# Output rows fetched and split by two threads, column groups in a new order, the bonus a thread of its own, value transposes of full width

## The chip, the cores and the metric

The kernel runs on one core of one Trainium2 chip. The metric is device time in microseconds of one execution; lower is better. A core has TensorE (PE; weight loads are shown apart as PEld), VectorE (DVE), ScalarE (ACT), GpSimd (POOL) and SyncE (SP), whose queue issues the DMAs here. The engines run side by side, each its own instructions in a fixed order, and wait for one another through semaphores.

## The reference, cut to what matters

One layer works on 528 prompt tokens (16 of them meta tokens) and 8 short sequences of 8 tokens, 592 rows of 2048 columns in all. One projection feeds two branches:

```python
z = einsum('btd,dn->btn', x, w_in)            # 4 x 1024 + 128 columns (r,k,v,g, lora), then 4 x 1024 (q,k,v,g)
# branch A, 16 heads of 64 (RWKV-7), zs = z shifted and mixed:
S = S * w_t + sa (x) b_t + v_t (x) k_t ;  o_t = S r_t      # sa = S (-kk_t)
bonus = sum(r * k * r_k) * v
o_a = (group_norm(o) + bonus) * silu(g)
# branch B, 8 heads of 128 (retention): scores with decay, a state by blocks, group norm, silu gate
h = einsum('btc,cd->btd', concat(o_a, o_b), w_out)
y = layer_norm(ALPHA * x + h)
```

The final states and the last projected rows are outputs too. All is float32.

## The kernel before, in words

**Planner.** No order is written out by hand. Each piece of work is a Python generator (a "job") that records operations; `Order` keeps a clock for each engine, prices every operation (`Engine.cost`, `TensorEngine`), and decides when it is emitted. The projection and output matmuls are emitted in a plain loop; behind each of them `pump` looks through the jobs by priority and emits those operations whose data are ready by the planner's clocks. For TensorE, data of other engines count as ready `LAG + SLACK` after their end (`SLACK` = 100 ns). `ensure` and `force` emit whatever is next when the loop needs something that is not there yet. So prices and slack only move instructions; they are no instructions themselves.

**Projection.** Rows of the input stand transposed in XH (leading part) and XL (rest), weights are split alike into wh and wl, and each product is three matmuls (wh by XH, wh by XL, wl by XH). A unit is 128 columns of `w_in`; it has two halves of tokens (272, 258 or 256, then 320), each 48 matmuls into one of two banks (`pj`). The list `units` has a first unit L (lora), then for each of 8 pairs p (two A heads, one B head): A k r v g, B q k v g. `gen_evac` empties the banks in that order, one half after the other, and waits there until the pair before has read the buffer that it writes. Splitting weights is ACT (wh) and DVE (wl), by `gen_split`.

**A heads.** `gen_a(p)` makes decays (a DVE scan, line 673), keys and the products within chunks of 64 tokens (ten chunks; the two heads' halves of the array side by side), then transposes k, then v chunk by chunk: ten transposes of 64 columns (line 760), with three evictions for each group of chunks. It then makes the bonus (`BD` products, added into zsV), and only then waits for the inverse of `gen_u(p)` (through DRAM: lt_d, tt_d) and runs the recurrence `gen_c` over nine chunks: three products a step, with evictions between. `gen_s(p)` is the part of the short sequences, `gen_f(p)` the normalization, bonus, gate and the row's write to o_d. **B heads** are `gen_b(h)`.

**Output.** The rows of o_d are fetched into five buffers (TH, E1, E2, TA, Z0 in turn), split into xo and xl (in the place of XH and XL) by `gen_o`, and multiplied with `w_out` in 64 steps. The first 14 steps take two token tiles only (six matmuls of 512 columns). `gen_o` is one thread: it waits once for the last pair (inverse, state products, bonus, evictions), then in turn splits row k and fetches row k+5.

## Time and profile before

| | |
|---|---|
| three runs | 1344.74, 1345.04, 1347.03 us (median 1345.04) |
| the profiled execution | 1345.04 us, its span 1343.3 us |
| busy | PE 1309.4 us, PEld 1230.2, DVE 879.8, ACT 634.4, POOL 55.3 |
| DMA | 139.82 MB, mean 104 GB/s |

The span runs from the first to the last instruction of the program; about 1.7 us lie around it. Busy is the union of an engine's instructions. A float32 matmul leaves two records, a split product or a transpose one. Matmuls are pipelined: the record of one overlaps the next, so the cost of one is the distance between starts, and an idle time of TensorE shows only where it is longer than that overlap. PE and DVE operations are recorded through helpers, so nearly all have the lines 380 (DVE, ACT, POOL), 403 (matmul), 409 (transpose) and 420 (DMA issue); in the changed kernel these are two lines further down.

### The profile page before, as it was taken

How to read it: one execution, taken by the hardware profiler on the slowest of the kernel's cores; microseconds unless marked ns; L12 is line 12 of the kernel's file. 1: busy time of each engine (PE TensorE's matmuls, PEld its weight loads, DVE VectorE, ACT ScalarE, POOL GpSimd, SP SyncE). 2: the span in 40 equal slices, each digit the busy share in tenths (PEclk: the TensorE clock that was granted, in tenths of full speed). 3: DMA queues.
4: the chain of work that ended last, by engine and by line, in shares of the span. 5: the costliest groups of instructions: out<-in, count | busy, mean ns of one | idle time of the engine just before them, and what ended most of it. 6: DMA issues, size and time to landing. Idle time of an engine off the chain costs nothing.

```text
span 1343.3 us, 27153 instructions
## 1 busy us (share of the span) xinstructions
PE 1309.4 (97%) x10488; PEld 1230.2 (92%) x10488; DVE 879.8 (65%) x2168; ACT 634.4 (47%) x1505; POOL 55.3 (4%) x117
## 2 busy tenths in 40 slices
PE   6999999999999999999999999999999998999995
PEld 6999999999999999999999999999999995777774
DVE  5765587658765876587658765876587658634258
ACT  4543654365536553655365536553655375512110
POOL 0000010000000010001000100010001000000002
PEclk9999999999999999999999999999999999999998
DMA  8343234322433243324332433243324356563224
GB/s 244 89 110 84 68 89 120 83 82 74 119 84 83 74 116 86 84 74 114 87 84 74 113 88 85 73 113 86 86 74 114 83 162 191 172 193 118 79 67 145
DMA packets 232344, 139.82 MB, mean 104 GB/s; under 512 B 58668, under 2 KB 212102, under 8 KB 231238
## 3 DMA queue, kind: packets, MB, share of 16 engines
q1 hardware_dynamic: 232214, 138.08, 36.2%
q8 instruction: 82, 1.34, 0.4%
q14 instruction: 48, 0.39, 0.1%
HBM read 119.30 MB, written 18.74 MB: 103 GB/s over the span
## 4 chain that ended last, share of the span: by engine, by line
PE 92%; DVE 5%; issue 1%; ACT 1%; DMA 0%; DVEq 0%; SPq 0%; ACTq 0%
PE bank L403 88%; PE bank L409 4%; DVE RW L380 3%; DVE wl L380 1%; DVE XL L380 1%; DMA RW<-in_x_prompt_dram 0%; DVE SHT L380 0%; ACT XH L380 0%; DVE XH L380 0%; ACT RT L380 0%; DVE RT L380 0%; ACT RSv L380 0%; ACT wh L380 0%; ACT SF L380 0%; ACT RHS L380 0%
## 5 line engine op out<-in xcount | busy, mean ns | idle before, releaser
L403 PE MATMUL bank<-XL,wh 128*128 128x320 f32 (+3 forms) x2080 | 631.3, 303 | 0.0
L403 PE MATMUL bank<-XH,wh 128*128 128x320 f32 (+3 forms) x2080 | 629.6, 303 | 1.2 <-ACT wh L380 1.2
L403 PE MATMUL bank<-XH,wl 128*128 128x320 f32 (+3 forms) x2080 | 626.1, 301 | 0.6 <-DVE wl L380 0.6
L403 PEld LDWEIGHTS bank<-XH,wh 128*128 128x128 f32 x2080 | 391.8, 188 | 3.6 <-ACT wh L380 1.4
L403 PEld LDWEIGHTS bank<-XH,wl 128*128 128x128 f32 x2080 | 392.0, 188 | 2.9 <-DVE wl L380 0.8
L403 PEld LDWEIGHTS bank<-XL,wh 128*128 128x128 f32 x2080 | 391.8, 188 | 2.9
L380 DVE TENSOR_TENSOR wl<-raw,wh 128x512 fp32r<-128x512 f32 x292 | 200.8, 689 | 156.2 <-ACT wh L380 151.8
L380 ACT ACTIVATE wh<-raw 128x512 fp32r<-128x512 f32 x292 | 183.8, 630 | 172.9 <-PE bank L403 145.6
L380 DVE TENSOR_TENSOR RW<-RW 120x84 f32<-120x84 f32 (+26 forms) x544 | 137.9, 256 | 18.5 <-DMA RW<-lt_d 4.1
L403 PE MATMUL bank<-RW 32*32 32x32 f32 (+6 forms) x2000 | 137.0, 239 | 4.8 <-DVE RW L380 4.7
L403 PEld LDWEIGHTS bank<-RW 32*32 32x32 f32 (+4 forms) x2000 | 109.8, 144 | 23.5 <-DVE RW L380 9.7
L380 ACT ACTIVATE RW<-bank 64x256 f32<-64x256 f32 (+8 forms) x218 | 93.2, 438 | 52.8 <-PE bank L403 29.1
L380 ACT ACTIVATE RT<-bank 64x320 f32<-64x320 f32 (+9 forms) x122 | 47.7, 397 | 114.0 <-DVE RT L380 72.6
L403 PE MATMUL bank<-more,XH 128*128 128x512 f32 (+1 forms) x250 | 75.9, 395 | 0.0
L380 ACT ACTIVATE SF<-RW,FT 64x64 f32<-64x64 f32 x144 | 49.4, 343 | 54.7 <-DVE RW L380 52.9
L403 PE MATMUL bank<-wh,XH 128*128 128x512 f32 x157 | 61.8, 396 | 0.0
L403 PE MATMUL bank<-wl,XH 128*128 128x512 f32 (+1 forms) x157 | 61.7, 395 | 0.0
L409 PE MATMUL bank<-CT,RW 128*128 128x128 f32 (+2 forms) x348 | 53.4, 283 | 8.3 <-DMA RW<-in_x_prompt_dram 7.6
L403 PEld LDWEIGHTS bank<-more,XH 128*128 128x128 f32 (+1 forms) x250 | 45.6, 183 | 12.6
L380 ACT ACTIVATE RW<-bank,OMM 128x272 f32<-128x272 f32 (+1 forms) x66 | 33.3, 504 | 45.6 <-PE bank L403 42.9
L403 PE MATMUL bank<-wh,XL 128*128 128x512 f32 x126 | 50.4, 400 | 1.4 <-DVE XL L380 1.4
L409 PEld LDWEIGHTS bank<-CT,RW 128*128 128x128 f32 (+2 forms) x348 | 42.0, 140 | 9.5 <-issue 7.6
(151 smaller groups left out, 1352.9 us busy)
## 6 DMA issues: line engine op xcount, KB each, us to landing
raw<-in_w_in_dram SPq DMA_DIRECT2D x259, 256.0 KB
raw<-in_w_out_dram SPq DMA_DIRECT2D x48, 256.0 KB
CT<-in_w_out_dram SPq DMA_DIRECT2D x30, 256.0 KB
RT<-in_state_ret_dram SPq DMA_DIRECT2D x8, 512.0 KB
out_dram<-RT SPq DMA_DIRECT2D x8, 512.0 KB
RW<-in_x_prompt_dram SPq DMA_DIRECT2D x16, 256.0 KB
out_dram<-RW SPq DMA_DIRECT2D x16, 256.0 KB
RW<-o_d SPq DMA_DIRECT2D x14, 288.0 KB
```

Of the source, the lines that this page charges most:

```text
L380: self.order.submit(Op(self.key, self.cost(name, n, kw, psum), reads, [out], lambda: f(*args, **kw)))
L403: lambda: self.eng.matmul(out, lhsT, rhs, start=start, stop=stop), (passes, move, load, shape, tiles)))
L409: lambda: self.eng.transpose(out, in_, ident), (1, move, _cols(in_) / 1.2, shape, tiles)))
```

## The change

- **Value transposes.** Five transposes of 128 columns (two chunks at a time) in two groups instead of ten of 64 in three; the chunks then lie in the two halves of the partitions, and each group is emptied by six evictions.
- **Bonus.** It becomes the job X{p}, started behind the transposes; the recurrence no longer waits for it. Readers wait for it: the addition in `gen_f` and the eviction of the next pair's r. A new mark V{p} tells the state part that the values are in place.
- **Column groups.** Ak Ar Bq Bk Bv Bg Av Ag, in the last pair Ak Ar Bq Av Bk Bv Ag Bg.
- **Fetch and split.** `gen_fetch` issues each row's fetch when its own buffer is free (TH, E1, E2 after the inverse, TA after the state products, Z0 after all evictions), `gen_o` splits.
- **Planner.** SLACK 200; a DVE operation costs 82 instead of 68 ns ahead of its elements, a scan twice as much per element, ACT 68 and 107 instead of 51 and 93.
- `gen_shift` also waits for all evictions.

```diff
@@ -29,7 +29,7 @@
 NPAIR = 8
 RAW_BUFS = 3
 HI_BUFS = 4
-SLACK = 100.0
+SLACK = 200.0
 AHEAD = -300.0
 RUN = 1200.0
 DRAIN = 90.0
@@ -44,6 +44,8 @@
 TURN = (4, 0, 1, 2, 3)
 LATE = 5
 EARLY = 14
+TURNS = "Ak Ar Bq Bk Bv Bg Av Ag"
+TURNS_LAST = "Ak Ar Bq Av Bk Bv Ag Bg"
 KEEP = ("A", 7, "g")
 BACKLOG = {0: 4000.0, 1: 1000.0, 2: 500.0, 3: 300.0, 4: 100.0}
 
@@ -356,10 +358,10 @@
 
     def cost(self, name, n, kw, psum):
         if self.key == "DVE":
-            return 68 + n * (6.3 if name == "reciprocal" else 1.04) + 57 * sum(
+            return 82 + n * {"reciprocal": 6.3, "tensor_tensor_scan": 2.08}.get(name, 1.04) + 57 * sum(
                 _is_ap(kw.get(k)) for k in ("scalar", "scalar1", "scalar2"))
         if self.key == "ACT":
-            return (51 if psum else 93) + n * 0.833 + 93 * sum(_is_ap(kw.get(k)) for k in ("scale", "bias"))
+            return (68 if psum else 107) + n * 0.833 + 93 * sum(_is_ap(kw.get(k)) for k in ("scale", "bias"))
         if kw.get("op") == ALU.pow:
             return 150 + n * 190.0
         if name == "memset":
@@ -752,16 +754,27 @@
         yield from prev(("F", 99))
         G.memset(Y[0:64, 0, 9, :], 0.0)
         G.memset(Y[64:128, 1, 9, :], 0.0)
-        for c0, c1 in ((0, 4), (4, 8), (8, 10)):
+        for g0, g1 in ((0, 4), (4, 5)):
             bb, = yield from take()
-            b = bb.rearrange("p (c n) -> p c n", c=4)
-            n = c1 - c0
-            for c in range(c0, c1):
-                T.transpose(b[0:64, c - c0, :], zsV[:, 64 * c:64 * c + 64], ident)
-            act(ZZ[64:128, c0:c1], b[0:64, 0:n].rearrange("p c (h v) -> p c h v", h=2))
-            act(Y[64:128, 0, c0:c1, :], b[0:64, 0:n, 0:64])
-            act(Y[0:64, 1, c0:c1, :], b[0:64, 0:n, 64:128])
+            b = bb.rearrange("p (g n) -> p g n", g=4)
+            for g in range(g0, g1):
+                T.transpose(b[:, g - g0, :], zsV[:, 128 * g:128 * g + 128], ident)
+            for e in range(2):
+                own, cs = b[64 * e:64 * e + 64, 0:g1 - g0], slice(2 * g0 + e, 2 * g1, 2)
+                act(ZZ[64:128, cs], own.rearrange("p g (h v) -> p g h v", h=2))
+                act(Y[64:128, 0, cs, :], own[:, :, 0:64])
+                act(Y[0:64, 1, cs, :], own[:, :, 64:128])
             give(bb)
+        mark(f"V{p}", 1)
+        od.call(lambda: od.start(f"X{p}", gen_bonus(p), 2))
+        yield from until((f"U{p}", 99))
+        b, = yield from take()
+        yield from gen_c(p, b)
+        give(b)
+        od.call(lambda: od.start(f"F{p}", gen_f(p), 2))
+        yield
+
+    def gen_bonus(p):
         yield from hold()
         b0, b1 = yield from take(2)
         for b, (c0, n) in zip((b0, b1), halves):
@@ -773,13 +786,6 @@
             tt(zsV[:, c0:c0 + n], b[:, :n], zsV[:, c0:c0 + n])
         release()
         give(b0, b1)
-        mark(name, 3)
-        yield
-        yield from until((f"U{p}", 99))
-        b, = yield from take()
-        yield from gen_c(p, b)
-        give(b)
-        od.call(lambda: od.start(f"F{p}", gen_f(p), 2))
         yield
 
     def gen_c(p, b):
@@ -879,6 +885,7 @@
                 if e == 0:
                     act(on[ro, 512:576], tr[0:64, 64 * h:64 * h + 64], ACTF.Identity, sc[ri], bi[ri])
         give(tr)
+        yield from until((f"X{p}", 99))
         tt(on, on, zsV[:, 64:640], ALU.add)
         stt(on, on, 0.5, zsG[:, 64:640])
         if p < NPAIR - 1:
@@ -908,6 +915,7 @@
                         m4[64 * e:64 * e + 64, :, 2 * h + r, :])
         T.transpose(n0[:, 256:384], RSv.rearrange("p r b t -> p (r b t)"), ident)
         act(RSs, n0[:, 256:384])
+        yield from until((f"V{p}", 1))
         mm(n0[:, 384:512], AR_[:, 1728:1856], Y[:, :, 9, :])
         tt(RHSs[0:64, 0:64], n0[0:64, 384:448], RSs[0:64, 0:64], ALU.add)
         tt(RHSs[64:128, 64:128], n0[64:128, 448:512], RSs[0:64, 64:128], ALU.add)
@@ -1060,7 +1068,7 @@
                         mark("lora", 1)
                 elif kind == "A":
                     if half == 0 and p:
-                        yield from until((f"A{p-1}", 1 if s == "k" else 3) if s in "kr" else (f"F{p-1}", 99))
+                        yield from until({"k": (f"A{p-1}", 1), "r": (f"X{p-1}", 99)}.get(s, (f"F{p-1}", 99)))
                     zs, i = {"r": (zsR, 0), "k": (zsK, 1), "v": (zsV, 2), "g": (zsG, 3)}[s]
                     evac_shift(units[ui], zs, 8 * i + p, half, b)
                 else:
@@ -1094,7 +1102,7 @@
 
     units = [("L", 0, "")]
     for p in range(NPAIR):
-        units += [("A", p, s) for s in "krvg"] + [("B", p, s) for s in "qkvg"]
+        units += [(x[0], p, x[1]) for x in (TURNS if p < NPAIR - 1 else TURNS_LAST).split()]
 
     def col0(u):
         kind, p, s = u
@@ -1263,26 +1271,37 @@
         obank = [(sq, pj[0], pj[1], r0, r1, m0, m1, ob)[i % 8] for i in range(len(cells))]
         trows = lambda t: 128 if t < 4 else 64
 
+        def gen_fetch():
+
+            for i in range(KO - 2):
+                t, kt = otk[i % 5], korder[i]
+                if t is TA:
+                    yield from until((f"S{NPAIR-1}", 1))
+                elif t is Z0:
+                    yield from until(("evac", 2 * len(units)))
+                else:
+                    yield from until((f"U{NPAIR-1}", 2))
+                if i >= 5:
+                    yield from until(("o", i - 4))
+                yield from until((f"{'F' if kt < 8 else 'B'}{kt % 8}", 99))
+                S.dma_start(out=t[:, 0:576], in_=o_d[kt])
+                mark("fetch", i + 1)
+                yield
+
         def gen_o():
 
-            yield from until((f"U{NPAIR-1}", 2), (f"S{NPAIR-1}", 1), (f"A{NPAIR-1}", 3), ("evac", 2 * len(units) - 8))
-
-            for ki in range(KO + 5):
-                if ki >= 5:
-                    k = ki - 5
+            for k in range(KO):
+                if k < KO - 2:
+                    yield from until(("fetch", k + 1))
                     t = otk[k % 5][:, 0:576]
-                    if k >= KO - 2:
-                        yield from until((f"B{NPAIR-1}", 99), (f"{'F' if k == KO - 1 else 'B'}{NPAIR-1}", 99))
-                        t = Y_[:, 64:640] if k == KO - 1 else ron
-                    yield from until(("event", n_in - 4 + min(3, (640 * k + 639) // TOK // 4) + 1))
-                    act(xo[:, k, 0:576], t)
-                    tt(xl[:, k, 0:512], t[:, 0:512], xo[:, k, 0:512].bitcast(F32), ALU.subtract)
-                    tt(xo[:, k, 576:640], t[:, 512:576], xo[:, k, 512:576].bitcast(F32), ALU.subtract)
-                    mark("o", k + 1)
-                if ki < KO - 2:
-                    kt = korder[ki]
-                    yield from until((f"{'F' if kt < 8 else 'B'}{kt % 8}", 99))
-                    S.dma_start(out=otk[ki % 5][:, 0:576], in_=o_d[kt])
+                else:
+                    yield from until((f"X{NPAIR-1}", 99), (f"B{NPAIR-1}", 99), (f"{'F' if k == KO - 1 else 'B'}{NPAIR-1}", 99))
+                    t = Y_[:, 64:640] if k == KO - 1 else ron
+                yield from until(("event", n_in - 4 + min(3, (640 * k + 639) // TOK // 4) + 1))
+                act(xo[:, k, 0:576], t)
+                tt(xl[:, k, 0:512], t[:, 0:512], xo[:, k, 0:512].bitcast(F32), ALU.subtract)
+                tt(xo[:, k, 576:640], t[:, 512:576], xo[:, k, 512:576].bitcast(F32), ALU.subtract)
+                mark("o", k + 1)
 
         def gen_xin():
             yield from until((f"F{NPAIR-1}", 99))
@@ -1337,7 +1356,7 @@
         xsamp_y = y_sample.rearrange("b t d -> (b t) d")
 
         def gen_shift():
-            yield from until((f"B{NPAIR-1}", 99))
+            yield from until((f"B{NPAIR-1}", 99), ("evac", 2 * len(units)))
             rows = SHO.rearrange("p s i -> p (s i)")
             for g, (c0, n) in enumerate(((0, 33), (33, 88), (121, 88), (209, 88))):
                 T.transpose(r0[0:n, 128 * g:128 * g + 128], rows[:, c0:c0 + n], ident)
@@ -1353,6 +1372,7 @@
             S.dma_start(out=lnb, in_=ln_b[0].partition_broadcast(128))
             yield
 
+        od.start("fetch", gen_fetch(), OPRIO)
         od.start("o", gen_o(), OPRIO)
         od.start("shift", gen_shift(), 4)
         od.start("ln", gen_ln(), 4)
```

TensorE has 40 instructions fewer (9072 for 9112); all others are the same in number and kind, in another order. Three places follow.

VectorE, fifth pair, around the scan of the decays (RW<-CT,RW 128x657). N is the eviction that the recurrence's next product waits for, wl a weight split. Before:

```order
L380 TENSOR_SCALAR RW<-RW 128x657
L380 SCALAR_TENSOR_TENSOR RT<-RT 128x576
L380 SCALAR_TENSOR_TENSOR RW<-CT,RW 128x657
L380 COPY MID<-RW 128x9
L380 TENSOR_TENSOR RW<-RW,MID 128x585
L380 TENSOR_TENSOR wl_107<-raw_100,wh_103 128x512
L380 TENSOR_TENSOR RW<-bank_118,N_78 64x128
L380 TENSOR_TENSOR wl_108<-raw_101,wh_104 128x512
```

Now:

```order
L382 TENSOR_SCALAR RW<-RW 128x657
L382 SCALAR_TENSOR_TENSOR RW<-CT,RW 128x657
L382 TENSOR_TENSOR wl_108<-raw_101,wh_104 128x512
L382 COPY MID<-RW 128x9
L382 TENSOR_TENSOR RW<-RW,MID 128x585
L382 TENSOR_TENSOR RW<-bank_118,N_78 64x128
L382 TENSOR_TENSOR wl_109<-raw_99,wh_105 128x512
```

The split has moved from behind the scan's followers to right behind the scan; an operation of the B head (RT) no longer stands ahead of it.

TensorE, fifth pair, the products within chunks (bank<-RW) among projection matmuls. Before:

```order
L403 MATMUL bank_118<-RW 128x128
L403 MATMUL bank_119<-RW 128x128
L403 MATMUL bank_115<-XH,wh_105 128x272
L403 MATMUL bank_118<-RW 128x128
L403 MATMUL bank_119<-RW 128x128
L403 MATMUL bank_118<-RW 128x128
L403 MATMUL bank_115<-XL,wh_105 128x272
```

Now:

```order
L405 MATMUL bank_116<-XH,wl_108 128x320
L405 MATMUL bank_119<-RW 128x128
L405 MATMUL bank_118<-RW 128x128
L405 MATMUL bank_119<-RW 128x128
L405 MATMUL bank_118<-RW 128x128
L405 MATMUL bank_119<-RW 128x128
L405 MATMUL bank_118<-RW 128x128
L405 MATMUL bank_119<-RW 128x128
L405 MATMUL bank_118<-RW 128x128
L405 MATMUL bank_116<-XH,wh_104 128x320
```

The first piece shows the last two of five, one projection matmul and the remaining three; now eight stand together.

TensorE, start of the output, at the state products of the last pair (64x32). Before, they stand in the last projection unit:

```order
L403 MATMUL bank_115<-XH,wl_109 128x256
L403 MATMUL bank_117<-RHS,RW 66x128
L403 MATMUL bank_118<-RW 64x32 x8
L403 MATMUL bank_116<-XH,wh_102 128x320
L403 MATMUL bank_117<-RW 128x128
```

Now, among output matmuls (wl by XH, wh by XH, 128x512):

```order
L405 MATMUL bank_115<-wl_108,XH 128x512
L405 MATMUL bank_117<-RW 64x32 x8
L405 MATMUL bank_118<-RW 128x128 x2
L411 MATMUL bank_117<-CT,RSv 128x128
L405 MATMUL bank_118<-RHS,RW 66x128
L405 MATMUL bank_117<-RW 128x128
L405 MATMUL bank_118<-RW 128x128
L405 MATMUL bank_117<-RW 66x128
L405 MATMUL bank_118<-RW 128x128
L405 MATMUL bank_117<-RW 128x128
L405 MATMUL bank_119<-wh_105,XH 128x512
```

They have moved behind the eighteenth output matmul; eight products of the last pair's state part and recurrence (and one transpose, RSv) follow without an output matmul between, and the next output matmul reads the fourth row.

## The prediction, made before the changed kernel was run

> **What bounds the kernel now.** I read the page first (busy shares, slices, chain), then TensorE alone by stage, then the places where its pitch breaks.
>
> ```profile
> span 1343.3 us, 27153 instructions
> PE 1309.4 (97%) x10488; PEld 1230.2 (92%) x10488; DVE 879.8 (65%) x2168; ACT 634.4 (47%) x1505; POOL 55.3 (4%) x117
> PE   6999999999999999999999999999999998999995
> PEclk9999999999999999999999999999999999999998
> PE 92%; DVE 5%; issue 1%; ACT 1%; DMA 0%; DVEq 0%; SPq 0%; ACTq 0%
> ```
>
> TensorE is busy in every slice at full granted clock, and the chain that ended last is TensorE for 92% of the span. So a matmul taken away is worth its pitch, and a wait of any other engine is worth only what TensorE stands still for it. There are two exceptions: slice 34, where TensorE drops (the change from projection to output), and the tail, which the change leaves alone. One pair of heads in the steady state, then a projection unit with no side work, then the last projection unit and the first 96 output matmuls:
>
> ```profile
> 544.00:678.60 134.60, 134.15 (x1178) 130.19 (x1177) 92.56 (x242) 69.81 (x172) 5.36 (x11) 1.00 0.33 90
> 1037.58:1050.28 12.70, 12.70 (x99) 12.70 (x97) 11.59 (x43) 4.04 (x8) 0.00 (x0) 1.00 0.31 89
> 1077.87:1101.20 23.33, 23.26 (x241) 22.27 (x239) 11.29 (x31) 16.63 (x51) 0.21 (x1) 1.00 0.54 154
> 1101.20:1143.07 41.87, 35.19 (x230) 25.96 (x229) 36.89 (x85) 27.24 (x62) 1.75 (x2) 1.00 0.64 193
> 1148.85 152.58 PE bank L403 x658
> ```
>
> The columns are the length, then PE, PEld, DVE, ACT and POOL busy with counts, the clock, the DMA share and GB/s. In the pair TensorE idles 0.45 us. The last row is from the chain: undisturbed output matmuls take 152.58/658 = 0.232 us each, so the 96 in the fourth row need 22.3 of its 41.87 us. The rest is side work and waiting, and there DVE is busy 88% of the time.
>
> **The value transposes.** Ten transposes of 64 columns per pair become five of 128. The group of the first, a stretch with four of them, and a stretch with four whole ones:
>
> ```profile
> L409 PE MATMUL bank<-CT,RW 128*64 128x128 f32 x88 | 14.8, 272 | 0.0
> 622.26 0.28 PE L403 MATMUL bank<-XH,wl 128*128 128x258 f32 x1
> 622.38 0.60 PE L409 MATMUL bank<-CT,RW 128*64 128x128 f32 x4
> 622.74 0.36 PE L403 MATMUL bank<-XH,wh 128*128 128x258 f32 x1
> 622.94 0.28 PE L403 MATMUL bank<-XL,wh 128*128 128x258 f32 x1
> 619.25 0.29 PE L403 MATMUL bank<-XL,wh 128*128 128x258 f32 x1
> 619.38 0.60 PE L409 MATMUL bank<-CT,RW 128*128 128x128 f32 x4
> 619.73 0.36 PE L403 MATMUL bank<-XH,wl 128*128 128x258 f32 x1
> 619.93 0.28 PE L403 MATMUL bank<-XH,wh 128*128 128x258 f32 x1
> ```
>
> The 88 are 80 of these and 8 in the output normalization. From the start of the projection matmul before to that of the second after pass 0.68 us in both stretches. Two projection matmuls of 258 columns take 0.12 each of it (622.26 to 622.38), so four transposes cost 0.44, half or whole: 0.11 us each. 40 fewer are worth 40 x 0.11 = **4.4 us**. Bounds: 4.0 (if the pitch in a shorter batch is 0.10) to 4.8 (0.12). The Trainium skill, "TensorEngine Tiling (Array Packing)", section Tiling Modes, speaks against this: it says that a stationary of 128x64 is one of two tiles that can work side by side, by which ten halves would cost what five wholes do and the change would save nothing here. The trace disagrees, since four halves took the same 0.44 us as four wholes, and this rule would put the time 4.4 us later.
>
> The evictions behind them go from nine to twelve per pair, with the same elements. The 24 more cost ACT at most 24 x 0.27 = 6.4 us by the smallest such row:
>
> ```profile
> L380 ACT ACTIVATE RW<-bank 64x128 f32<-64x128 f32 x2 | 0.5, 265 | 0.0
> ```
>
> I cost them at nothing, because ACT is idle 65 of the 134.6 us of a pair and the recurrence that reads these values starts 13 projection matmuls (13 x 0.145 = 1.9 us) behind the last of these transposes. Were that cover gone, it would be 0.8 per pair.
>
> **The intra-chunk products kept together.** In six pairs before (p2 to p7) eight chunks' products (two heads' 64x128 halves side by side, two records for each) are cut five and three around one projection matmul. In the new order all but the first pair have them in eights.
>
> ```profile
> 604.80 0.29 PE L403 MATMUL bank<-XH,wl 128*128 128x272 f32 x1
> 605.02 0.93 PE L403 MATMUL bank<-RW 64*128 64x128 f32 x10
> 605.88 0.39 PE L403 MATMUL bank<-XH,wh 128*128 128x272 f32 x1
> 606.20 0.71 PE L403 MATMUL bank<-RW 64*128 64x128 f32 x6
> 606.84 0.39 PE L403 MATMUL bank<-XL,wh 128*128 128x272 f32 x1
> 607.07 0.29 PE L403 MATMUL bank<-XH,wl 128*128 128x272 f32 x1
> 611.08 0.31 PE L403 MATMUL bank<-XH,wh 128*128 128x320 f32 x1
> 611.32 1.16 PE L403 MATMUL bank<-RW 64*128 64x128 f32 x16
> 612.41 0.42 PE L403 MATMUL bank<-XL,wh 128*128 128x320 f32 x1
> 612.66 0.32 PE L403 MATMUL bank<-XH,wl 128*128 128x320 f32 x1
> ```
>
> Cut: 607.07 - 604.80 = 2.27, less three projection matmuls of 0.125, is 1.90. Whole: 612.66 - 611.08 = 1.58, less two of 0.145, is 1.29. The difference of about 0.58, less one new cut of five in the first pair, makes 6 x 0.58 = **3.5 us**, bounds 2.5 to 3.5. Otherwise the new order has some two side batches more per pair (62 for 60). A batch costs the sum of its members in the rows above, so I take nothing for that; at the 0.08 by which the matmul behind a batch is late (622.74 to 622.94) 16 more would be 1.3.
>
> **The stall behind the scan.** The planner priced the scan (line 673 of the code) as any 657-column operation; it now gets double per element. What happened in the fifth pair, and its trace in the chain of six pairs (first and last):
>
> ```profile
> 577.82 1.52 DVE L380 TENSOR_TENSOR_SCAN RW<-CT,RW 128x657 f32<-128x657 f32 x1
> 580.98 0.28 DVE L380 TENSOR_TENSOR RW<-bank,N 64x128 f32<-64x128 f32 x1
> 580.57 0.30 PE L403 MATMUL bank<-XH,wh 128*128 128x320 f32 x1
> 581.32 0.49 PE L403 MATMUL bank<-RW 128*128 128x128 f32 x2 [0.45 <-DVE RW L380]
> 311.08 0.61 DVE wl L380
> 984.19 0.61 DVE wl L380
> ```
>
> The recurrence's product waits in TensorE's queue for a DVE operation that stands behind the scan and a weight split. Starts 0.75 us apart instead of 0.145 make 0.6 lost, about what the scan exceeds the planner's old price by; six pairs make **3.6 us**. DVE needs 581.26 - 577.82 = 3.4 us from the scan's start to that operation's end. In the new order the same operations stand there (the weight split right behind the scan), but 24 projection matmuls instead of 18 between the scan's place and the product: 24 x 0.145 = 3.5 us and about 1 us of side products. I count the stall as gone. Bounds: it stays (0) or gone (3.6).
>
> Smaller waits of that recurrence are left:
>
> ```profile
> PEld bank L403 <- DVE RW L380: 9.7, 20, 1.6
> ```
>
> The row (total, times, longest) is weight loads that wait for DVE; a good part is at the change to output, and most is covered by the matmul before. With 100 ns more slack for everything TensorE waits for I take **1.5 us** off; bounds -3.6 (a new stall of 0.6 in six pairs) to +3.
>
> **The change to the output.** Rows 3 and 4 of the stage table: 65.2 us in which 12.7 (the projection unit) and 22.3 are projection and output; I price the side batches by pitches as above at 20.0, so TensorE stands still for 10.2. Now the retention head of the last pair is done a unit earlier, since its gate comes last alone, and its DVE work no longer meets the output splits: DVE instructions placed within the first 96 output matmuls go from 83 to 73. Against that, three row fetches go out ahead of the loads that return the inverse (TT), and the last inverse's products come some 35 projection matmuls later. The fourth row's buffer (TA) is freed by the state products, now only 18 matmuls into the output. So in the new order TensorE has there one batch of dependent products, behind which output matmul 19 waits for a fetch:
>
> ```profile
> 1092.80 4.36 SPq L420 DMA_DIRECT2D RW<-o_d  x3
> 1095.25 0.67 ACT L380 ACTIVATE XH<-RW 128x576 fp32r<-128x576 f32 x1
> L380 ACT ACTIVATE RSv<-bank x8: 177/190/195, 1092.9 to 1099.1; 64x32 f32<-64x32 f32 x8
> ```
>
> Issue to use took 2.45, the split 0.67. Beside them run eight evictions of 0.19, a weight split, and three round trips between TensorE and DVE or ACT, about 6.5 us in all by my count, for 2 us of TensorE's own work: 4.5 lost. With some 3 more spread over the stage the standing still is 7.5 instead of 10.2: **2.7 us** won. Bounds: -3 (it grows to 13) to +9 (1 us of waits is left).
>
> **The rest costs nothing.** The bonus as its own thread makes the next pair's receptance eviction wait for it (behind that wait stand all further evictions, and TensorE for their banks). Its last product stands 176 projection matmuls before that eviction, at 12.70/96 = 0.13 us some 23 us, which cover it. Values and gate now come seventh and eighth; their waits on the pair before (F) end three units earlier in the order.
>
> **Sum.** The profiled execution's own time is 1345.04 for a span of 1343.3, and also the median of the three runs. 1345.0 - 4.4 - 3.5 - 3.6 - 1.5 - 2.7 = 1329.3; forecast **1329**, its own range 1325 to 1333.5.
>
> **Rivals.**
> 1. The waits only change place: 4.4 + 3.5 are work that is gone, all else stays. 1337. For it: every part of the order has moved, and recurrences that meet other work stall anew. Against it: the new prices fit the rows.
> 2. The change to output is freed altogether (9 instead of 2.7): 1323. For it: DVE's 88% there, of which a fifth moves away. Against it: the batch behind which the fetch stands.
> 3. Slower: the last recurrence becomes the bound. It starts later, has nine steps of three products with round trips, and the fifteenth and sixteenth output rows need its end. If each step held TensorE for 2 us it would be 18 us, and with the work that is gone 1345.0 - 7.9 - 5.1 + 18 = 1350. It decides from about 1.4 us a step on. Against it: some 100 output matmuls (23 us) and the side work lie beside it.
> 4. The batch at the fourth row makes TensorE's clock drop. In the last of the 40 slices, where TensorE idles at the end, the granted clock is 0.8. If the next 48 output matmuls ran at half clock, 48 x 0.232 = 11.1 us more: 1340. Against it: in the fourth stage row TensorE idles 6.7 us in pieces up to 1.6 and the clock stays at 1.00. The Trainium skill, "TensorE: Matmul & The Clock Gate", Part 1, has the clock fall to half after an idle window of about 3.4 us; no stretch of this trace but the start and the tail is that idle, and the products strewn into the batch speak against an empty window.
> 5. The change does not pay: gains are eaten by new stalls of about 2.2 us in each of seven pairs; 1345.
>
> **Chances.** Forecast 0.60, rival 1 0.17, rival 2 0.12, rival 4 0.03, rival 5 0.04, rival 3 0.04. This kernel's measurement tells no less than about 0.2% (2.7 us) from no change. Faster 0.92, less some doubt in the work terms: 0.91; same 0.05; slower 0.04. Range 1321 to 1338, from rival 2 with a little beyond to rival 1 with a little beyond.
>
> **What would show it.** Right: 40 fewer transposes, pairs of 132.4 to 133.2 us instead of 134.6, no DVE weight split in the chain once per pair, the first 96 output matmuls some 4 us shorter, with one wait of several us at the fourth row. Wrong: pairs of 133.5 and more (rival 1), or that stage longer than before (rival 3).

## The result, and the profile after

The changed kernel takes 1326.12 us (median of four runs, 1324.99 to 1327.4) against 1345.15 us for the kernel before; the ratio is 0.9856, with a 95% interval of 0.9839 to 0.9873. That is 19.0 us less; the forecast was 1329, 16 us less. The profiled execution took 1324.99 us.

The page of the changed kernel, the lines that answer to those of before:

```profile
span 1323.2 us, 27055 instructions
PE 1296.7 (98%) x10448; PEld 1226.0 (93%) x10448; DVE 879.0 (66%) x2168; ACT 636.5 (48%) x1529; POOL 56.0 (4%) x117
PE   7999999999999999999999999999999999999995
PE 95%; DVE 3%; issue 1%; ACT 1%; DMA 0%; SPq 0%; DVEq 0%; ACTq 0%
```

TensorE has 40 fewer matmuls, the dip of slice 34 has gone, and the chain is TensorE for 95% of the span where it was 92%.

By stage (columns: stretch and its length, then PE, PEld, DVE, ACT and POOL busy with counts, granted clock, DMA share, GB/s): the same pair of heads, the last projection unit, and the first 96 output matmuls.

```profile
553.30:685.54 132.24, 132.24 (x1173) 129.41 (x1173) 91.97 (x241) 70.10 (x176) 5.66 (x11) 1.00 0.34 91
1065.50:1082.40 16.90, 16.27 (x180) 15.43 (x179) 13.69 (x29) 9.97 (x25) 1.53 (x3) 1.00 0.49 139
1082.40:1120.50 38.10, 35.57 (x199) 28.09 (x197) 29.84 (x74) 29.64 (x74) 0.00 (x0) 0.96 0.69 211
```

The pair takes 132.24 us, just under the 132.4 to 133.2 that was to show the forecast right (134.60 before). The first 96 output matmuls take 38.1 instead of 41.87, as said some 4 us less. Their granted clock is 0.96, and that was not in the forecast.

The waits of TensorE's weight loads (total, times, longest), one row of before that the prediction had left out, then two of the changed kernel:

```profile
PEld bank L403 <- ACT RHS L380: 5.0, 11, 1.5
```

```profile
PEld bank L405 <- DVE RW L382: 2.4, 3, 1.8
PEld bank L405 <- ACT RHS L382: 1.1, 3, 0.7
```

Waits for DVE fell from 9.7 us in 20 to 2.4 us in three, those for ACT's copies of the recurrence from 5.0 to 1.1: 11.2 us together, a part of it covered by the matmul before. A second account is of the same size. Take the distances between the starts of the projection and output matmuls, take off their pitches (0.145, 0.12, 0.232 us) and the side batches by the prices of the prediction; what is left is TensorE standing still. It was 25.9 us over the program and is 14.3: 7.4 less in the pairs before the last, 4.1 less in the last pair with the output stage. The side batches themselves went from 241.5 to 233.7 us, 7.8 less, the 4.4 and 3.5 of the prediction within 0.1. As the account takes the prediction's own prices, this says only that the batches are those that were foreseen. The starts show the price itself; here are the five value transposes of the fifth pair in the changed kernel, each group with the projection matmul behind it:

```profile
671.14 0.60 PE L411 MATMUL bank<-CT,RW 128*128 128x128 f32 x4
671.49 0.36 PE L405 MATMUL bank<-XH,wl 128*128 128x258 f32 x1
674.72 0.27 PE L411 MATMUL bank<-CT,RW 128*128 128x128 f32 x1
674.75 0.37 PE L405 MATMUL bank<-XH,wh 128*128 128x258 f32 x1
```

They put the projection back by 0.35 and 0.03 us, and the matmul behind each group is late by another 0.08: 0.54 us. The ten halves of the kernel before stand in three groups, which take 0.35, 0.36 and 0.14 us and three times 0.08: 1.09 us. The difference, 0.55 us in each of eight pairs, is the 4.4.

The two stalls that the prediction named in the fifth pair, in the timeline of the changed kernel (start, duration, engine, operation): the scan with the DVE operation that the recurrence waits for and TensorE's product behind it, then a group of products within chunks:

```profile
570.70 1.53 DVE L382 TENSOR_TENSOR_SCAN RW<-CT,RW 128x657 f32<-128x657 f32 x1
573.90 0.28 DVE L382 TENSOR_TENSOR RW<-bank,N 64x128 f32<-64x128 f32 x1 [0.21 <-PE bank L405]
574.78 0.38 PE L405 MATMUL bank<-RW 128*128 128x128 f32 x2
...
601.92 1.16 PE L405 MATMUL bank<-RW 64*128 64x128 f32 x16
```

The DVE operation still ends 3.5 us behind the scan's start (574.18 - 570.70), but the product comes 0.6 us later and waits for nothing. The eight products stand together. In the chain of the changed kernel no DVE weight split is left behind a scan; in the kernel before one stood there in each of six pairs.

And the place of the fourth row in the output stage, the timeline and then three stretches of it:

```profile
1089.61 0.33 SPq L422 DMA_DIRECT2D RW<-o_d  x1
1091.70 0.49 PE L405 MATMUL bank<-RW 128*128 128x128 f32 x2 [1.63 <-DVE RW L382]
1093.67 0.68 ACT L382 ACTIVATE XH<-RW 128x576 fp32r<-128x576 f32 x1 [0.62 <-DMA RW<-o_d]
```

```profile
1088.07:1091.49 3.42, 2.00 (x24) 1.36 (x22) 2.49 (x6) 3.33 (x13) 0.00 (x0) 1.00 0.63 160
1091.49:1094.90 3.41, 2.30 (x11) 1.34 (x11) 1.47 (x7) 2.36 (x8) 0.00 (x0) 1.00 0.87 236
1094.90:1098.32 3.42, 3.42 (x11) 2.93 (x12) 3.08 (x9) 1.53 (x5) 0.00 (x0) 0.50 1.01 375
```

The wait stands where it was predicted: between output matmuls at 1088.67 and 1095.78 lie 7 us for some 2 us of TensorE's own work. Behind it the granted clock is half for 3.41 us, and two output matmuls start 0.43 us apart there (1096.35 and 1096.78) instead of 0.23. By the clock alone, what TensorE did in that stretch would have taken some 1.7 us less at full clock (an estimate).

### The profile page after: what moved, and what is told of

Same layout as the page of the kernel before. It is cut to its first block, busy times and chain, and to the rows that moved or that the text cites. A ratio compares the mean times of both kernels' runs of the same rounds, so it can differ in the third digit from the quotient of the medians.

```text
span 1323.2 us, 27055 instructions
## 1 busy us (share of the span) xinstructions
PE 1296.7 (98%) x10448; PEld 1226.0 (93%) x10448; DVE 879.0 (66%) x2168; ACT 636.5 (48%) x1529; POOL 56.0 (4%) x117
## 4 chain that ended last, share of the span: by engine, by line
PE 95%; DVE 3%; issue 1%; ACT 1%; DMA 0%; SPq 0%; DVEq 0%; ACTq 0%
PE bank L405 91%; PE bank L411 4%; DVE RW L382 2%; DMA RW<-in_x_prompt_dram 0%; DVE SHT L382 0%; DVE XL L382 0%; ACT wh L382 0%; DVE wl L382 0%; ACT XH L382 0%; ACT RSv L382 0%; DVE MOM L382 0%; SPq L422 0%; ACT RT L382 0%; ACT SF L382 0%; ACT RHS L382 0%
## 5 line engine op out<-in xcount | busy, mean ns | idle before, releaser
L405 PE MATMUL bank<-RW 32*32 32x32 f32 (+6 forms) x2000 | 132.8, 237 | 2.0 <-DVE RW L382 1.9
L382 ACT ACTIVATE RW<-bank 128x320 f32<-128x320 f32 (+9 forms) x242 | 94.9, 410 | 55.7 <-PE bank L405 36.5
L411 PE MATMUL bank<-CT,RW 128*128 128x128 f32 (+3 forms) x308 | 47.6, 283 | 7.8 <-DMA RW<-in_x_prompt_dram 7.4
L382 DVE SCALAR_TENSOR_TENSOR RW<-RW 128x576 f32<-128x576 f32 (+4 forms) x72 | 39.7, 576 | 12.2 <-PE bank L405 11.5
```

The lines of the kernel that those rows point to most:

```text
L382: self.order.submit(Op(self.key, self.cost(name, n, kw, psum), reads, [out], lambda: f(*args, **kw)))
L405: lambda: self.eng.matmul(out, lhsT, rhs, start=start, stop=stop), (passes, move, load, shape, tiles)))
L411: lambda: self.eng.transpose(out, in_, ident), (1, move, _cols(in_) / 1.2, shape, tiles)))
```

## The experiments

Each group ran beside runs of the kernel before (1346.58, 1346.0 and 1345.51 us). The changed kernel itself was not run again there; by its ratio 0.9856 it stands at 1327.2, 1326.6 and 1326.1, and "the changed kernel" below means these. The ratios have intervals of about 0.0013 to either side, and that of the changed kernel 0.0017, so a difference between two variants is sure to some 2.5 us, and one between a variant and the changed kernel to some 3 us.

### Half-width transposes put back

```diff
-            T.transpose(b[:, g - g0, :], zsV[:, 128*g:128*g + 128], ident)   # five, six evictions a group
+            T.transpose(b[0:64, c - c0, :], zsV[:, 64*c:64*c + 64], ident)   # ten, as before
```

> The changed kernel with ten half-width value transposes per pair again, nothing else undone. Theory (a transpose costs its pitch of 0.11 us, whole or half): 40 x 0.11 = 4.4 us more, 1330.5. Rival (halves overlap in two column tiles): no difference, 1326.1. The chunk products stay in eights in its order, so no other term should move.

Measured 1333.12 us, ratio 0.99 [0.9886, 0.9913]: 5.9 us above the changed kernel. The rival, no difference, is out. By the account above the side work grows by 4.36 us, which is the predicted 4.4; the remaining 1.5 us are within what can be told apart. The two profiles lie further apart than the medians, 8.7 us: 5.8 in the eight pairs, 1.7 before the first pair, where this profile has a stretch at half clock and that of the changed kernel has none, and 0.9 in the first 96 output matmuls, with half clock for 6.83 us instead of 3.41. The price of the transposes is right.

### Whole transposes alone, in the kernel before

The same lines changed in the kernel before, and nothing else.

> The kernel before with whole value transposes alone (bonus still in line, old prices, old column order, one output thread). Theory: 4.4 us for 40 transposes and about 2.9 for chunk products that stand uncut in its order in all but one pair; the scan's stall and the change to the output as before: 1337.8. Rival (the transposes are hidden or overlap): 1342.

Measured 1348.24 us, ratio 1.0011 [1.0003, 1.002]: nothing is won, and both expectations were missed. The work is 7.2 us less (the products within chunks happen to stay together here too), but TensorE stands still 37 us instead of 25.9, for 6.8 in the second pair and some 2 to 3 in each later one, and twice the clock is half behind a stall. In the second pair it is this:

```profile
218.51 0.39 PE L403 MATMUL bank<-XH,wh 128*128 128x258 f32 x1 [1.26 <-ACT RW L380]
```

A projection matmul with all its data there waits for ACT, that is, for its bank to be emptied. That the work taken away counts only as far as the new order of everything else allows was rival 1's argument, and here it decides.

### The old order of columns in the changed kernel

```diff
-TURNS = "Ak Ar Bq Bk Bv Bg Av Ag"
-TURNS_LAST = "Ak Ar Bq Av Bk Bv Ag Bg"
+TURNS = TURNS_LAST = "Ak Ar Av Ag Bq Bk Bv Bg"
```

> The changed kernel with the old order of column groups (r k v g of A, then q k v g of B, in all pairs). Theory (the new order pays at the change to the output, where the last retention head no longer meets the output splits; in the pairs it is neutral): pairs stay at 132.2 us, the first 96 output matmuls go back towards 41.9 us from 38.1, 1330 to 1332. Rival (the new order helps in every pair): pairs longer by 0.5 us and more, 1333 and more. Second rival (the order is worth nothing): 1326.

Measured 1382.39 us, ratio 1.0276 [1.0261, 1.0291]: 56 us slower than the changed kernel, and 36 slower than before. The rival that the new order helps in every pair holds by its open bound (1333 and more), but nothing had led me to expect this size. TensorE stands still 6.5 to 7.9 us in every pair but the first, always at the end of the value's unit and the start of the gate's, and the clock is half for 6.83 us behind it (3.41 in one pair). The output stage is longer too, as the theory had it: the first 96 output matmuls take 46.6 us instead of 38.1, with half clock for 10.24 us.

### The scan's price alone, in the kernel before

```diff
-            return 68 + n * (6.3 if name == "reciprocal" else 1.04) + 57 * ...
+            return 68 + n * {"reciprocal": 6.3, "tensor_tensor_scan": 2.08}.get(name, 1.04) + 57 * ...
```

> The kernel before with one edit: the planner prices a scan at 2.08 ns per element instead of 1.04. Theory (the once-per-pair stall of 0.6 us came from this price): the stall goes, 3.6 to 4.5 us; in its order the chunk products also stand uncut in eights, 3.5 us; together 1337.5. Rival (the stall comes from the weight split or from the old slack of 100 ns): the stall stays, only the cuts go, 1341.6.

Measured 1379.58 us, ratio 1.0242 [1.0228, 1.0256]: 33 us slower than before, by one number in a price list. Both expectations, 1337.5 and 1341.6, were missed, and yet what the theory said of the stall behind the scan is so: that stall is gone in all six pairs. In the fifth pair the DVE operation that the recurrence waits for now stands ahead of the scan, and the product comes without a wait:

```profile
588.33 0.28 DVE L380 TENSOR_TENSOR RW<-bank,N 64x128 f32<-64x128 f32 x1
588.53 1.51 DVE L380 TENSOR_TENSOR_SCAN RW<-CT,RW 128x657 f32<-128x657 f32 x1
591.75 0.38 PE L403 MATMUL bank<-RW 128*128 128x128 f32 x2
```

What the price costs is another stall, at the same place as in the run above. Its stretches in the fifth pair, and then TensorE's timeline and its waits in all:

```profile
633.03:636.44 3.41, 1.89 (x15) 1.30 (x14) 3.23 (x9) 0.76 (x2) 0.00 (x0) 1.00 0.39 112
636.44:639.85 3.41, 1.98 (x8) 1.50 (x8) 2.14 (x7) 2.40 (x6) 0.00 (x0) 0.50 0.80 200
639.85:643.27 3.42, 3.42 (x18) 3.42 (x17) 0.77 (x1) 0.00 (x0) 0.29 (x2) 0.50 0.48 159
```

```profile
638.63 0.58 PE L403 MATMUL bank<-XH,wh 128*128 128x258 f32 x1 [1.14 <-ACT RW L380]
```

```profile
PE bank L403 <- ACT RW L380: 7.6, 7, 1.1
```

Seven waits of a first projection matmul for ACT, one in each pair but the first: again a bank that is not emptied. These 1.1 us are the smaller part of the stall. Ahead of them, since the bank is not free, the planner emits the transposes of the keys, and those wait for DVE (2.7 us here). The eviction that should empty it is the value's first half, which has to wait until the pair before has been normalized (F), since F still reads the old values. In this run F's last eviction, F's addition that reads the old values, and the value's eviction stand like this:

```profile
631.96 0.56 ACT L380 ACTIVATE RW<-bank,VEC 64x256 f32<-64x256 f32 x1
636.67 0.75 DVE L380 TENSOR_TENSOR RW<-RW 128x576 f32<-128x576 f32 x1
637.81 0.48 ACT L380 ACTIVATE RW<-bank,OMM 128x272 f32<-128x272 f32 x1
```

In the kernel before it stands like this (F's last eviction and the two operations of the value's, then TensorE's first matmul into the emptied bank):

```profile
613.14 0.56 ACT L380 ACTIVATE RW<-bank,VEC 64x256 f32<-64x256 f32 x1
616.16 0.49 ACT L380 ACTIVATE RW<-bank,OMM 128x272 f32<-128x272 f32 x1
616.55 0.39 ACT L380 ACTIVATE RW<-bank 128x272 f32<-128x272 f32 x1
```

```profile
618.05 0.28 PE L403 MATMUL bank<-XH,wh 128*128 128x258 f32 x1
```

The value's eviction is two operations and done at 616.94; TensorE is back at that bank at 618.05. So the margin between the two was some 1.1 us in this pair, and the pairs follow one order. With the dearer scan the planner puts the recurrence, and behind it F's transposes, 22 projection matmuls later (79 matmuls into the value's unit instead of 57): 22 x 0.145 = 3.2 us and the side work between them, more than the margin. In the changed kernel the value is the seventh group of columns, and the same eviction comes far behind F (F's last eviction, the value's):

```profile
614.10 0.56 ACT L382 ACTIVATE RW<-bank,VEC 64x256 f32<-64x256 f32 x1
661.15 0.49 ACT L382 ACTIVATE RW<-bank,OMM 128x272 f32<-128x272 f32 x1 [4.66 <-PE bank L405]
```

### That theory tested: value and gate fifth, value and gate fourth

Two more orders of columns in the changed kernel, which differ only in whether B's k stands ahead of the value and gate or behind them.

```diff
-TURNS = "Ak Ar Bq Bk Bv Bg Av Ag"
+TURNS = "Ak Ar Bq Bk Av Ag Bv Bg"     # value fifth
+TURNS = "Ak Ar Bq Av Ag Bk Bv Bg"     # value fourth
```

> The changed kernel with the columns of the value fifth and of the gate sixth (k r q k v g v g: the pairs' order is Ak Ar Bq Bk Av Ag Bv Bg; the last pair as in the change). Theory (the eviction of the value's first half waits for the normalization of the pair before, F; the old order is slow with the new prices because F then comes after it): here the transposes of F stand at unit 2 + 92 matmuls and the value's first half ends at unit 4 + 48, 148 projection matmuls (some 21 us) later, so no stall: 1325 to 1330, rest per pair under 1.2 us, no halved clock in the pairs. Rival (the stall comes from something else in the old neighbourhood of value, gate and the state's columns, of which most is back here): 1345 to 1380.

> The changed kernel with value and gate one place earlier than in the run before (Ak Ar Bq Av Ag Bk Bv Bg; only one group of columns has changed its place). Theory: the recurrence is placed later too, the transposes of F stand at unit 3 + 86 matmuls, 38 behind the end of the value's first half at unit 3 + 48; evictions and TensorE wait for F in every pair, the clock halves: 1365 to 1390, with the standing still in units 3 and 4 instead of 2 and 3. Rival (something else in the old order): under 1340, as the columns that came between are the new order's.

Value fifth: 1328.55 us, ratio 0.9873 [0.9859, 0.9886]; 1.4 us of standing still per pair (a little over the 1.2 expected), no half clock in the pairs. Value fourth: 1360.67 us, ratio 1.0115 [1.0101, 1.0128]; 32 us slower by one group of columns. Between the two profiles some 21 us of it lie in the pairs, where the stall is in units 3 and 4 (up to 7.5 us a pair) and the clock half for 6.83 us in three of the seven. Some 9 us more lie in the first 96 output matmuls (43.9 us instead of 34.5, with half clock for 13.65 us), of which the theory did not speak; their cause stays open. The sum is a little less than the 1365 expected, since the first pairs hardly stall. The value's eviction in the first of these, then in the second kernel F's last eviction, the two evictions behind it, the value's, and TensorE:

```profile
634.26 0.49 ACT L382 ACTIVATE RW<-bank,OMM 128x272 f32<-128x272 f32 x1 [1.11 <-PE bank L405]
```

```profile
627.27 0.56 ACT L382 ACTIVATE RW<-bank,VEC 64x256 f32<-64x256 f32 x1
...
630.67 0.91 ACT L382 ACTIVATE RW<-bank 128x512 f32<-128x512 f32 x2 [1.37 <-PE bank L411]
631.59 0.49 ACT L382 ACTIVATE RW<-bank,OMM 128x272 f32<-128x272 f32 x1
```

```profile
632.41 0.58 PE L405 MATMUL bank<-XH,wh 128*128 128x258 f32 x1 [1.26 <-ACT RW L382]
```

Value fifth, the eviction waits only for TensorE's own products. Value fourth, it stands behind F (whose addition on DVE ends at 628.64) and the evictions that were placed in the meantime, and TensorE stands behind it. The theory held against the rival, which wanted the fourth place under 1340.

### Old prices and old slack; each alone

```diff
-            return 82 + n * {"reciprocal": 6.3, "tensor_tensor_scan": 2.08}.get(name, 1.04) + ...   # DVE
-            return (68 if psum else 107) + ...                                                     # ACT
-SLACK = 200.0
+            return 68 + n * (6.3 if name == "reciprocal" else 1.04) + ...
+            return (51 if psum else 93) + ...
+SLACK = 100.0
```

All of it in the changed kernel:

> The changed kernel with the planner's old prices and slack (68 ns, scan like any, 51 and 93, slack 100). Theory (prices and slack removed the waits inside pairs): pairs go back to about 133 us or more, 4 to 7 us more in all, 1330 to 1333. Rival (the waits went because of the new column order): pairs stay at 132.2, 1326.

The slack alone, then the scan's price alone:

> The changed kernel with the old slack of 100 ns, new prices kept. The old prices and the old slack together cost 14.8 us. Theory (the slack makes most of it, as the small waits of every round trip are planned with it): 1334 to 1341. Rival (the prices make it, the slack next to nothing, as the prediction had it with 1.5): 1327 to 1330.

> The changed kernel with the scan at the old price per element (0.7 us too little), other prices and slack as changed. By the prediction the stall behind the scan comes back in six or seven pairs: 1330.5 (1327 + 3.6). Rival (24 matmuls instead of 18 between the scan and the product leave room enough in the new order): 1326 to 1328. Other rival (any change of the plan breaks several places at once, as in the runs before): 1333 or more.

All: 1341.44 us, ratio 0.9966 [0.9954, 0.9979], 14.8 us more than the changed kernel; the expectation of 4 to 7 was too low. TensorE stands still 2.3 to 4.6 us in a pair instead of 0.6, in many small waits:

```profile
PEld bank L405 <- DVE RW L382: 7.2, 25, 0.6
```

The slack alone: 1334.46, ratio 0.9916 [0.9902, 0.9929], 8.3 us of the 14.8, which is the theory's side. Pairs stand still 2.15 us, of which 1.2 is one weight split that comes late, first on ACT (here), then on DVE:

```profile
634.64 0.19 PEld L405 LDWEIGHTS bank<-XH,wh 128*128 128x128 f32 x1 [0.64 <-ACT wh L382]
```

The scan's price alone: 1327.56, ratio 0.9865 [0.9852, 0.9879], 1.4 us more, within what can be told apart. So the stall behind the scan does not come back with the scan's old price alone; the product stands at least 22 projection matmuls behind the scan. But it is not the order of columns that keeps it away: in the run with all old prices and the old slack, which has the same new order, the weight load of a recurrence product waits again, in each of the six pairs, for the DVE operation behind the scan (0.3 to 0.6 us; this is the fourth pair, whose scan starts at 447.63):

```profile
451.00 0.30 PEld L405 LDWEIGHTS bank<-RW 128*128 128x128 f32 x2 [0.38 <-DVE RW L382]
```

The scan's price in the old order, or the slack with the other prices in the new one, removes that stall; with neither it stays. The other prices were not tried alone: of the 14.8 us some 5 are left to them and to what the parts do together.

### The output stage: two buffers exchanged, four buffers, one thread

```diff
-        otk = [TH, E1, E2, TA, Z0]
+        otk = [TH, E1, E2, Z0, TA]      # the fourth row no longer waits for the state part
```

> The changed kernel with two output-row buffers exchanged: the fourth row goes to Z0, free after the last eviction, the fifth to TA, freed by the state products. Theory (output matmul 19 stands behind the fetch into TA): most of the 6.3 us of standing still in the first 48 output matmuls goes, and with it the halved clock behind it: 1321 to 1322. Rival (TensorE stands still because the state part's and recurrence's products depend on one another, whatever the fetch): 1326.

Four buffers without TA, the fifth row then waiting for the first to be read:

```diff
-        otk = [TH, E1, E2, TA, Z0]
+        otk = [TH, E1, E2, Z0]          # and i % 4, o - 3 in the fetch
```

> The changed kernel with four output-row buffers: TA, freed by the state products, is not used at all. Theory of the fetch: as with the exchange of buffers or somewhat better, 1320.5 to 1322. Rival (four buffers starve the split, since a row is fetched only when one four rows back is split): 1323 to 1326.

Fetch and split in one thread again, all else as changed:

```diff
-        od.start("fetch", gen_fetch(), OPRIO)
+        # gen_o fetches five rows ahead and splits, as before
```

> The changed kernel with fetch and split of the output rows in one thread again, which waits for all of the last pair at once. Theory: now all rows, not the fourth alone, wait for the state products, which the new column order has put behind the start of the output: 3 to 6 us more, 1329 to 1332. Rival (the fourth row's wait decides either way): 1326.

Exchanged: 1325.42 us, ratio 0.9841 [0.9828, 0.9855], 1.8 us less than the changed kernel. No stretch at half clock is left there and the first 48 output matmuls take 21.4 us instead of 25.2, but dependent products of the last recurrence still hold TensorE:

```profile
1093.29 0.49 PE L405 MATMUL bank<-RW 128*128 128x128 f32 x2 [1.02 <-DVE RW L382]
```

Four buffers: 1326.2, ratio 0.9851 [0.9836, 0.9867], 0.4 us less. Both are nearer the rival than the theory. So the fetch behind the state part is worth some 2 us, not the 5 or 6 that I expected of taking it away; the round trips of the state part and the recurrence make the rest. One thread: 1328.92, ratio 0.9876 [0.9863, 0.989], 2.3 us more, a little under the 3 to 6 expected, with a stall in the last projection unit and the clock half for 13.65 us behind it:

```profile
1085.51 0.43 PE L405 MATMUL bank<-RHS,RW 128*66 128x128 f32 x2 [1.39 <-ACT RHS L382]
```

None of the three can be told from the changed kernel with certainty; the one with the buffers exchanged is the fastest measured.

## Why the prediction was right, and where it was not

- **The work taken away (4.4 + 3.5).** Right: 7.8 us by the account of both traces, 4.4 for the transposes by their starts, and the half transposes cost 5.9 when they were put back. A slip in the second term is small: its own 1.90 and 1.29 differ by 0.61, not 0.58, and the new cut that it took off for the first pair is not in the trace, so it should have been 3.6. But the work is not a gain by itself: whole transposes alone won nothing in the kernel before (1348.24).
- **Twelve evictions for nine at no cost.** Right as far as shown: by the same account, in no pair of the changed kernel but the last does TensorE stand still more than 0.8 us.
- **The stall behind the scan (3.6).** It went, with 24 projection matmuls or more between scan and product, as the prediction counted. The cause that it named, the scan's price, is borne out as far as this stall goes: that price alone, in the old order, removes it in all six pairs. What the prediction did not see is that the price is not needed once slack and other prices are new (1327.56 us), and that alone, in the old order, it makes the kernel 33 us slower, since the later plan meets another limit.
- **Smaller waits of the recurrence (1.5).** Mis-sized. Together with the scan's stall 5.1 us were expected off the pairs, and 7.4 were measured. The prediction had the row of waits for DVE, 9.7 us, but not the row for ACT's copies, 5.0 us, which fell to 1.1. And the slack, counted inside these 1.5, is worth 8.3 us in the new order.
- **The change to the output (2.7).** The wait of several us stands at the fourth row, as predicted, and the size is 4.1. Of the two things that the prediction saw there, the fetch and the round trips beside it, the round trips hold TensorE longer: with the fetch no longer behind the state part the kernel wins only some 2 us. Without the half clock the stage would have won about 5.8.
- **Rival 4 (the clock drops behind that batch).** It was given 0.03 and 11.1 us. It happened, for 3.41 us instead of 48 matmuls, at a price of about 1.7. The argument against it, that products strewn into the batch prevent it, is refuted: TensorE was busy 2.00 and 2.30 of 3.4 us in the two stretches ahead of it. The Trainium skill, "TensorE: Matmul & The Clock Gate", Part 1, was cited for an idle window of about 3.4 us; the length of the window agrees with these stretches, but that it must be idle does not.
- **"The rest costs nothing."** This is the step that failed, though the time of the kernel does not show it. The order of columns was priced at nothing and mentioned for the waits on F ending three units earlier. It is what the rest stands on: the old order had 1.1 us of margin between the value's eviction, which has to wait for F, and TensorE's return to its bank. The scan's price alone passes it in every pair but the first, and the whole transposes alone in the second pair; slack and the other prices were not tried alone in the old order. Without the new order the rest of the change would have cost 36 us instead of winning 19. With the order alone and old prices (and all other parts of the change) the gain is 4.6 us.
- So the sum came within 3 us because its terms were read off the order of the whole changed kernel, in which all parts are present; the terms for the waits and for the output were both too small, and only the half clock, some 1.7 us, took a part of that back. As a statement on what each part is worth by itself, it was wrong for three of them: order, slack, scan's price.

## What to carry to other kernels

Before a planner's price or slack is changed, look for the resource whose margin is smallest (here a bank that is emptied 1.1 us before its next use, behind a reader of the pair before), since a later plan costs nothing until it passes that margin and then costs it in every round. Give that reader room first, by the order of the work, and then let the prices be cautious. Judge parts of such a change only together with the order that they rest on: the whole transposes were worth 4 to 6 us in the changed kernel and nothing in the kernel before, and the scan's price that removed a stall of 3.6 us cost 33 in all.

## What the runs showed of the hardware that was not expected

**The granted clock goes by stretches of 3.41 us, and TensorE need not be idle to lose it.** (Busy is the share of a stretch that TensorE's records cover, and their ends are modelled.) In every profile the stretches at half clock inside the program begin and end on one grid of 3.41 us and last 3.41, 6.83, 10.24 or 13.65 us. Inside the program the first half-clock stretch came behind one in which TensorE was busy for 28% to 70% of the time; no stretch under 56% was without it, and none over 70% brought it. Between these it went either way: the kernel before had 1.99 of 3.41 us (58%) without a drop (and one of 64% ahead of it), the changed kernel 67% with one.

```profile
1133.11:1136.52 3.41, 1.99 (x14) 1.49 (x12) 1.44 (x5) 2.79 (x7) 0.00 (x0) 1.00 0.40 121
1136.52:1139.94 3.42, 3.14 (x63) 2.58 (x65) 2.29 (x6) 1.76 (x5) 0.00 (x0) 1.00 0.38 96
```

What decides between these is open. Full clock mostly came back behind a stretch that was busy nearly throughout (92% and more in all cases but one of 85%); in the kernel with one thread three stretches of 86%, 87% and 68% were not enough, and it stayed at half for four (with the half transposes one of 93% was not enough):

```profile
1086.33:1089.74 3.41, 2.93 (x13) 2.30 (x13) 1.33 (x3) 1.89 (x7) 0.00 (x0) 0.50 0.45 150
1089.74:1093.16 3.42, 2.96 (x22) 2.18 (x22) 0.85 (x3) 0.87 (x3) 0.00 (x0) 0.50 0.87 285
1093.16:1096.57 3.41, 2.31 (x7) 1.28 (x7) 0.62 (x2) 3.20 (x14) 0.00 (x0) 0.50 0.57 174
1096.57:1099.99 3.42, 3.39 (x10) 2.80 (x10) 2.87 (x10) 1.83 (x4) 0.00 (x0) 0.50 0.51 125
```

So a stall of 2 us can cost up to 1.7 us more for each stretch at half clock behind it (half of 3.41, an estimate). In most of the experiments' profiles, though not in those of the two kernels compared, one such stretch also lies at the start, at about 18 us.

**A granted clock that costs nothing.** The kernel with the exchanged buffers shows 0.95 where the changed kernel shows 1.00, and the same number of TensorE's records within one in the same 132 us:

```profile
500.00:632.00 132.00, 132.00 (x1171) 129.12 (x1170) 91.88 (x239) 70.07 (x175) 5.65 (x11) 0.95 0.34 91
```

```profile
500.00:632.00 132.00, 132.00 (x1172) 129.15 (x1171) 91.52 (x240) 70.10 (x175) 5.66 (x11) 1.00 0.34 91
```

The first row is of the exchanged buffers, the second of the changed kernel. Why the record differs was not tried.
